# A decoder layer on one core: norm_mix as one row, spread over the partitions by two matmuls, and a written order for pre-norm and first projection

## Chip, cores and metric

One core of a Trainium2 chip runs the whole program. The metric is device time in microseconds (us) of one execution, as the median of several runs. TensorE is PE in the rows, VectorE DVE, ScalarE ACT, GpSimd POOL, SyncE SP.

## What is computed

A decoder layer on 512 tokens of width 1024, all in fp32. The part that matters here is its first line and the projection of it:

```python
def rms_norm(x, g):
    y = xf * lax.rsqrt(jnp.mean(xf * xf, axis=-1, keepdims=True) + NORM_EPS)
    return (y * g.astype(jnp.float32)).astype(x.dtype)
...
    xn = rms_norm(h, norm_mix[l])
    proj = xn @ w_in[l]                      # 1024 x 3128
    y_r = rwkv7_group(proj[..., :R_COLS], ...)
    y_n = nsa_group(proj[..., R_COLS:], positions, ...)
    h = h + jnp.concatenate([y_r, y_n], axis=-1) @ w_out[l]
    xn = rms_norm(h, norm_ffn[l])
    h = h + swiglu(xn, w_gate[l], w_up[l], w_down[l])
```

`rwkv7_group` is a linear recurrence over time in 8 heads; `nsa_group` is attention with compressed, selected and windowed keys, whose compression (`compress`) is a small MLP on blocks of 32 tokens: `silu(win @ w1 + b1) @ w2`. A final rms_norm ends the layer.

## The kernel before

Tokens lie in NT = 4 tiles of 128, the width in KB = 8 blocks of 128. Every fp32 operand of a product is split in a rounded high part (`split`: a copy on ACT to fp32r, L144) and the rest (a subtraction, on DVE at L146, or on POOL where asked), and `mm3` multiplies high by high, high by low and low by high (L163, L164, L165), so that a product of 128x512 is 3 matmuls for each block of the width.

The start: SP loads the first token tile in two halves, norm_mix, the first half of the weights `raw0`, tile 1, the second half, tiles 2 and 3, and `raw1`. TensorE runs 10 matmuls on the identity (WARM, L250) that nobody reads. For each token tile, `norm_transposed` sums the squares (ACT L173, L176), takes the root (L177), the reciprocal (DVE L178), multiplies the tile by it and by `gain` (norm_mix on all 128 partitions; one scalar_tensor_tensor, here STT, at L190; two of 512 columns for tile 0), transposes it block by block into two PSUM banks of tag "s" (PE L194), and splits each bank into `xh` (ACT) and `xl` (DVE). `proj_tok` then multiplies the tile by the 256 columns of w0, 24 matmuls of 256 columns. In this text T0 to T3 are the transposes of the four tiles, P0 to P3 these products, xh(1) the high parts of tile 1. After them the products of the remaining columns of w_in (128x512) follow, with the jobs that use them; among these are the sigmoids of `lora` products (L400 and L401 multiply, ACT L402 applies the sigmoid, DVE L405 scans), the sine and cosine of the rotary angles (ACT L360, L361), and `job_cmp1`, the first layer of the compression (DVE L660, ACT L661, DVE L662 make its operand `win`, PE L666 multiplies). The FFN combines blocks of w_gate and w_up by sums before it multiplies (`block4`, L1141 to L1145, with loads that add on arrival, issued by POOL).

A scheduler decides the order of the instructions on each engine at build time, from the order of the code, from its own estimates and from `tc.high_priority()`; on the chip each engine runs its list in order. A block `tc.manual_schedule(engines=...)` keeps the order of the code for the engines named. So an edit at the start changes the scheduler's lists also where the code is the same.

Of the kernel before, what the change touches and what calls it, by code (L numbers as in the profile page):

```python
# [17 lines left out]
S, D = 512, 1024  # L18
# [28 lines left out]
def hybrid_layer(ctx: ExitStack, tc: tile.TileContext, x, positions, norm_mix, w_in, mu_shift, w0, w2, a0, a2,  # L47
# [15 lines left out]
    def st(shape, tag, bufs=1, dtype=F32):  # L63
        return sb.tile(list(shape), dtype, name=tag, tag=tag, bufs=SB_BUFS.get(tag, bufs))
# [25 lines left out]
    gain = st([128, D], "t4")  # L90
# [4 lines left out]
    nc.sync.dma_start(gain, bcast_row(norm_mix))  # L95
# [85 lines left out]
    def norm_transposed(src, gain, hT, lT, halves=False):  # L181

        xn2 = st([128, 2, D], "b8")
        for t in range(NT):
            s = src(t)
            cut = (slice(0, 512), slice(512, D)) if halves and t == 0 else (slice(0, D),)
            r = rstd_of(s, cut)
            xn = xn2[:, t % 2]
            for c in cut:
                DVE.scalar_tensor_tensor(xn[:, c], s[:, c], r, gain[:, c], op0=OP.mult, op1=OP.mult)  # L190
            for k0 in range(0, KB, 4):
                p = ps("s")
                for k in range(4):
                    PE.transpose(p[:, k * 128:(k + 1) * 128], xn[:, (k0 + k) * 128:(k0 + k + 1) * 128], ident)  # L194
                pv = p.rearrange("p (k n) -> p k n", n=128)
                sl = slice(t * 128, (t + 1) * 128)
                split(pv, hT[:, k0:k0 + 4, sl], lT[:, k0:k0 + 4, sl])
            yield

# [49 lines left out]
    for _ in range(WARM):  # L249
        PE.matmul(idle[:, 0:128], ident, ident, start=True, stop=True)  # L250
    ident2 = st([128, 64], "ident2")
# [43 lines left out]
    norm = norm_transposed(lambda t: xt[:, t], gain, xh, xl, True)  # L295
    ctok = st([128, NT, 4, 64], "t4")
    for t in range(NT):
        next(norm)
        if t == 0:
            w0p = parts(raw0)  # L300
        ACT.activation(ctok[:, t].rearrange("p h d -> p (h d)"), proj_tok(w0p, t), AF.Copy)
    w1p = parts(raw1, lo_pool=True)
# [953 lines left out]
    for n, (a, b) in enumerate(GROUPS):  # L1256
        one, two = halves[n]
        a11, a21, a12, a22 = (h[:, :, x] for h in (one, two) for x in (left, right))
        first, last = n == 0, n == 1
        t1, t2 = block4(a, 0, "wraw"), block4(b, 1, ("gin", "kB")[n])  # L1260
        t3 = st([128, 4, 512], "wraw") if first else None
        t3 = [t3[:, 2 * i:2 * i + 2] if first else st([128, 2, 512], "t4") for i in range(2)]
# [4 lines left out]
        multiply(m1, a_side(a11), b_side(t1), first, last)  # L1267
# [7 lines left out]
        multiply(m5, a_side(a21), b_side(t1), first, last)  # L1275
# [84 lines left out]
```

## Time and profile before

| | |
|---|---|
| median of 3 runs | 760.38 us (759.34 to 761.85) |
| the profiled execution, its own time | 762.32 us |
| its span in the trace | 760.6 us |
| mean granted clock of TensorE | 0.981 of full |
| TensorE busy | 726.2 us, 95% |
| DVE, ACT, POOL busy | 593.1, 399.1, 164.6 us |

The span is what the trace shows of the profiled execution; the timed runs are other executions. Busy shares are of the span.

### The profile page before, as it was taken

The numbers are of one execution on the slowest core, as the hardware profiler recorded it, in microseconds if no ns is written. First come the engines' busy times: TensorE is split into PE (matmuls) and PEld (weight loads), VectorE is DVE, ScalarE is ACT, GpSimd is POOL, SyncE is SP. The second block draws the span as 40 slices with busy tenths as digits, with TensorE's granted clock in tenths as the row PEclk, the third lists the DMA queues.
The fourth block names the chain that finished last, engine by engine and source line by source line (L and its number), as shares of the span: only waits on it lengthen the run. The fifth ranks groups of instructions, "written<-read, shape, count | busy, mean of one in ns | idle before, by whom it ended". The sixth has DMA issues, their size and how long they took to land.

```text
span 760.6 us, 14951 instructions
## 1 busy us (share of the span) xinstructions
PE 726.2 (95%) x6045; PEld 636.6 (84%) x6045; DVE 593.1 (78%) x1089; ACT 399.1 (52%) x666; POOL 164.6 (22%) x262
## 2 busy tenths in 40 slices
PE   6999999998879999999998699999999999999996
PEld 6967878898867888767787699999999999877885
DVE  5488688879868888786459496969688789999835
ACT  6398735324366866756437534535344454465424
POOL 3210053048435542454001101111102001010000
PEclk7999999999999999999998999999999999999999
DMA  7723533100061000230415747695967629443302
GB/s 249 198 85 110 166 111 110 57 2 2 3 222 30 2 2 2 58 112 1 139 56 139 165 130 177 155 229 145 225 161 194 143 81 272 172 110 111 139 0 110
DMA packets 73467, 87.02 MB, mean 114 GB/s; under 512 B 4996, under 2 KB 62934, under 8 KB 73398
## 3 DMA queue, kind: packets, MB, share of 16 engines
q1 hardware_dynamic: 60694, 72.43, 29.2%
q0 software_dynamic: 12704, 13.63, 11.6%
q8 instruction: 47, 0.77, 0.4%
q14 instruction: 22, 0.18, 0.1%
HBM read 83.96 MB, written 2.10 MB: 113 GB/s over the span
## 4 chain that ended last, share of the span: by engine, by line
PE 67%; DVE 22%; DMA 4%; issue 3%; ACT 3%; POOL 0%; SPq 0%; DVEq 0%; ACTq 0%
PE ps_ra L164 6%; PE ps_ra L165 6%; PE ps_ra L163 6%; PE ps_pj L165 6%; PE ps_pj L163 6%; PE ps_pj L164 6%; PE ps_o L1001 3%; PE ps_s L165 3%; PE ps_s L163 3%; PE ps_s L164 3%; DVE wlo L146 3%; DVE L L146 3%; PE ps_pj L993 3%; DMA L<-in_w_up_dram 2%; DVE whi L146 2%
## 5 line engine op out<-in xcount | busy, mean ns | idle before, releaser
L144 ACT ACTIVATE whi<-wraw 128x1024 fp32r<-128x1024 f32 (+1 forms) x63 | 62.5, 1030 | 36.0 <-issue 9.1
L146 DVE TENSOR_TENSOR wlo<-wraw,whi 128x1024 fp32r<-128x1024 f32 (+1 forms) x46 | 58.9, 1306 | 16.3 <-ACT whi L144 12.8
L165 PE MATMUL ps_ra<-L,wlo 128*128 128x512 f32 (+2 forms) x144 | 50.9, 355 | 0.0
L990 POOL TENSOR_SCALAR whi<-whi,m,gates 128x128 f32<-128x128 f32 (+3 forms) x64 | 42.5, 680 | 37.1 <-DVE m L988 28.8
L164 PE MATMUL ps_ra<-L,whi 128*128 128x512 f32 (+2 forms) x136 | 47.4, 348 | 1.1 <-DVE L L146 1.1
L163 PE MATMUL ps_ra<-L,whi 128*128 128x512 f32 (+2 forms) x136 | 47.0, 346 | 1.2 <-ACT L L144 1.2
L164 PE MATMUL ps_pj<-L,whi 128*128 128x512 f32 (+1 forms) x128 | 45.7, 357 | 0.0
L163 PE MATMUL ps_pj<-L,whi 128*128 128x512 f32 (+1 forms) x128 | 45.1, 357 | 0.0
L165 PE MATMUL ps_pj<-L,wlo 128*128 128x512 f32 (+1 forms) x120 | 41.2, 343 | 0.0
L987 ACT ACTIVATE whi<-whi,m 128x128 f32<-128x128 f32 (+3 forms) x64 | 35.4, 554 | 9.5 <-DVE m L986 8.3
L163 PE MATMUL ps_ra<-whi,L 128*128 128x256 f32 (+1 forms) x108 | 35.7, 332 | 0.2 <-ACT L L144 0.2
L164 PE MATMUL ps_ra<-wlo,L 128*128 128x256 f32 (+1 forms) x108 | 35.7, 330 | 0.2 <-DVE wlo L146 0.2
L165 PE MATMUL ps_ra<-whi,L 128*128 128x256 f32 (+1 forms) x108 | 35.1, 327 | 0.0
L986 DVE CUSTOM_DVE_ANT_0 whi<-ps_s,negb 128x128 f32<-128x128 f32 (+3 forms) x64 | 29.3, 484 | 5.9 <-PE ps_pj L993 2.5
L165 PE MATMUL ps_pj<-whi,L 128*128 128x256 f32 (+1 forms) x108 | 33.9, 315 | 0.0
L164 PE MATMUL ps_pj<-wlo,L 128*128 128x256 f32 (+1 forms) x108 | 33.8, 313 | 0.0
L163 PE MATMUL ps_pj<-whi,L 128*128 128x256 f32 (+1 forms) x108 | 33.6, 315 | 0.0
L1141 POOL DMA_DIRECT2D t<-in_w_up_dram x6 | 7.9, 1323 | 114.0 <-DVE whi L146 50.2
L165 PEld LDWEIGHTS ps_ra<-L,wlo 128*128 128x128 f32 (+1 forms) x144 | 27.2, 189 | 4.2 <-issue 0.5
L164 PEld LDWEIGHTS ps_ra<-L,whi 128*128 128x128 f32 (+1 forms) x136 | 25.6, 188 | 4.8 <-DVE L L146 1.3
L163 PEld LDWEIGHTS ps_ra<-L,whi 128*128 128x128 f32 (+1 forms) x136 | 25.7, 189 | 4.7 <-ACT L L144 1.4
L164 PEld LDWEIGHTS ps_pj<-L,whi 128*128 128x128 f32 x128 | 24.9, 195 | 3.4 <-DVE L L146 0.4
(685 smaller groups left out, 2561.2 us busy)
## 6 DMA issues: line engine op xcount, KB each, us to landing
wraw<-in_w_gate_dram SPq DMA_DIRECT2D x22, 512.0 KB
wraw<-in_w_in_dram SPq DMA_DIRECT2D x9, 1024.0 KB
wraw<-in_w_down_dram SPq DMA_DIRECT2D x9, 1024.0 KB
t<-in_w_up_dram POOLq DMA_DIRECT2D x12, 512.0 KB, 7.4
wraw<-in_w_up_dram SPq DMA_DIRECT2D x11, 512.0 KB
L<-in_w_up_dram POOLq DMA_DIRECT2D x10, 512.0 KB, 8.2
wraw<-in_w_out_dram SPq DMA_DIRECT2D x4, 1024.0 KB
wraw<-in_w_in_dram SPq DMA_DIRECT2D x6, 512.0 KB
```

The source lines that it names most:

```text
L144: ACT.activation(hi, src, AF.Copy)
L146: (POOL if pool else DVE).tensor_sub(lo, src, hi.bitcast(F32))
L163: PE.matmul(o, lh, rh, start=start, stop=False)
L164: PE.matmul(o, lh, rl, start=False, stop=False)
L165: PE.matmul(o, ll, rh, start=False, stop=stop)
L986: DVE.tensor_tensor_reduce(pr[:, i], pS[:, i], negb[:, S - n:S], scale=-1.0, scalar=3e38, op0=OP.add, op1=OP.min, accum_out=m[:, i, 0:1])
L987: ACT.activation(pr[:, i], pr[:, i], AF.Exp, scale=-1.0, bias=m[:, i, 0:1], accum_out=m[:, i, 1:2])
L990: POOL.tensor_scalar(pr[:, i], pr[:, i], m[:, i, 2:3], gv[:, 1 + b0 + i, h:h + 1], op0=OP.mult, op1=OP.mult)
L993: PE.transpose(pT[:, j], prr[:, x, j * 128:j * 128 + 128], ident)
L1001: PE.matmul(po[q, 2 * g:2 * g + 2], vtok[:, j % (t + 1), b0 + j // (t + 1), g], pTs[:, par, j], start=False, stop=g == 1 and bs[-1] == 1 a ...
L1141: POOL.dma_start(t1, quarter(w_up, 0), accum_op=OP.add)
```

## The change

`gain` is no longer loaded to all partitions (128 times 4 KB): one row of 4 KB is loaded, and two fp32 matmuls behind WARM multiply it by a row of 128 ones, which leaves norm_mix on all partitions in two PSUM banks, of tags "rb" and "o". The STT reads its second operand from there, and is cut in two halves of 512 columns for all tiles. The loop over `norm_transposed` becomes a block with a written order for ACT and DVE. The low parts of w1 (two of 1024 columns) are made by DVE and no longer by POOL. Two variables of the FFN get other names.

```diff
-    gain = st([128, D], "t4")
+    gain_row = st([128, D], "t4")[0:1]
+    one = st([128, 256], "rp")[0:1, 0:128]
+    POOL.memset(one, 1.0)
...
-    nc.sync.dma_start(gain, bcast_row(norm_mix))
+    nc.sync.dma_start(gain_row, bass.AP(tensor=norm_mix.tensor, offset=norm_mix.offset, ap=[[D, 1], [1, D]]))
...
     idle = ps("o")
     for _ in range(WARM):
         PE.matmul(idle[:, 0:128], ident, ident, start=True, stop=True)
+    gain = [ps(o) for o in ("rb", "o")]
+    for f in range(2):
+        PE.matmul(gain[f], one, gain_row[:, f * 512:f * 512 + 512], start=True, stop=True)
...
-    norm = norm_transposed(lambda t: xt[:, t], gain, xh, xl, True)
     ctok = st([128, NT, 4, 64], "t4")
-    for t in range(NT):
-        next(norm)
-        if t == 0:
-            w0p = parts(raw0)
-        ACT.activation(ctok[:, t].rearrange("p h d -> p (h d)"), proj_tok(w0p, t), AF.Copy)
-    w1p = parts(raw1, lo_pool=True)
+    def rstd(t):
+        r[t] = rstd_of(xt[:, t], (slice(0, 512), slice(512, D)) if t == 0 else ())
+
+    def normed(t):
+        xn = xn2[:, t % 2]
+        for f in range(2):
+            c = slice(f * 512, f * 512 + 512)
+            DVE.scalar_tensor_tensor(xn[:, c], xt[:, t, c], r[t], gain[f], op0=OP.mult, op1=OP.mult)
+            p = turned[t, f] = ps("s")
+            for k in range(4):
+                PE.transpose(p[:, k * 128:(k + 1) * 128], xn[:, (f * 4 + k) * 128:(f * 4 + k + 1) * 128], ident)
+
+    def parted(t):
+        for f in range(2):
+            ks, tl = slice(f * 4, f * 4 + 4), slice(t * 128, t * 128 + 128)
+            split(turned[t, f].rearrange("p (k n) -> p k n", n=128), xh[:, ks, tl], xl[:, ks, tl])
+
+    def weights0(f):
+        ks = slice(f * 4, f * 4 + 4)
+        split(raw0[:, ks], w0p[0][:, ks], w0p[1][:, ks])
+
+    with tc.manual_schedule(engines={mybir.EngineType.Activation, mybir.EngineType.DVE}):
+        rstd(0)
+        normed(0)
+        weights0(0)
+        parted(0)
+        rstd(1)
+        normed(1)
+        weights0(1)
+        rstd(2)
+        parted(1)
+        for t in range(NT):
+            p = proj_tok(w0p, t)
+            if t < 2:
+                normed(t + 2)
+                if t == 0:
+                    rstd(3)
+                parted(t + 2)
+                if t == 1:
+                    w1p = parts(raw1)
+            ACT.activation(ctok[:, t].rearrange("p h d -> p (h d)"), p, AF.Copy)
```

The change adds lines to the file, so lines of the new one are other numbers: L190 answers to L294 there, L194 to L297, L144/L146 to L146/L148, L163 to L165 become L165 to L167, and from L304 on the new number is 25 higher (L666 is L691, L1145 is L1170).

What the scheduler makes of it is shown at three places. First DVE's list from its fourth instruction on, at the start of the program; `cneg` is a mask that the attention uses much later, `cvalid` what POOL makes for it. Before:

```order
L178 RECIPROCAL ss<-ss 128x1
L190 SCALAR_TENSOR_TENSOR b_165<-L,ss,t_69 128x512 x2
L283 TENSOR_SCALAR cneg<-cvalid 128x128
L146 TENSOR_TENSOR wlo<-wraw,whi 128x1024
L146 TENSOR_TENSOR L<-ps_s,L 128x4x128 x2
L178 RECIPROCAL ss<-ss 128x1
L190 SCALAR_TENSOR_TENSOR b_165<-L,ss,t_69 128x1024
```

After:

```order
L180 RECIPROCAL ss<-ss 128x1
L269 TENSOR_SCALAR cneg<-cvalid 128x128
L294 SCALAR_TENSOR_TENSOR b_170<-L,ss,ps_rb 128x512
L294 SCALAR_TENSOR_TENSOR b_170<-L,ss,ps_o 128x512
L148 TENSOR_TENSOR wlo<-wraw,whi 128x1024
L148 TENSOR_TENSOR L<-ps_s,L 128x4x128 x2
L180 RECIPROCAL ss<-ss 128x1
L294 SCALAR_TENSOR_TENSOR b_170<-L,ss,ps_rb 128x512
L294 SCALAR_TENSOR_TENSOR b_170<-L,ss,ps_o 128x512
L148 TENSOR_TENSOR wlo<-wraw,whi 128x1024
```

`cneg` stands behind the first two STTs in the list before and ahead of them in the list of the change; the rest is the written order.

Second, PE's list around the second `lora` products (L400, L401 before; L425, L426 after; `t_517` and `t_529` are the same operand) and the first compress product (L666, L691, its operand `t_757`, `t_769`). Before, the four `lora` products and what follows:

```order
L400 MATMUL ps_s<-b_518,t_517 128x512
L401 MATMUL ps_s<-b_518,t_517 128x512
L400 MATMUL ps_s<-b_518,t_517 128x512
L401 MATMUL ps_s<-b_518,t_517 128x512
L163 MATMUL ps_pj<-L,whi 128x512
L164 MATMUL ps_pj<-L,whi 128x512
L163 MATMUL ps_ra<-L,whi 128x512
L164 MATMUL ps_ra<-L,whi 128x512
L165 MATMUL ps_pj<-L,wlo 128x512
```

and the first compress product, 45 rows further on:

```order
L165 MATMUL ps_ra<-L,wlo 128x512
L163 MATMUL ps_ra<-L,whi 128x512
L164 MATMUL ps_ra<-L,whi 128x512
L165 MATMUL ps_ra<-L,wlo 128x512
L666 MATMUL ps_o<-whi,t_757 128x256
L666 MATMUL ps_o<-wlo,t_757 128x256
```

After:

```order
L425 MATMUL ps_s<-b_530,t_529 128x512
L426 MATMUL ps_s<-b_530,t_529 128x512
L425 MATMUL ps_s<-b_530,t_529 128x512
L426 MATMUL ps_s<-b_530,t_529 128x512
L691 MATMUL ps_o<-whi,t_769 128x256
L691 MATMUL ps_o<-wlo,t_769 128x256
```

The first compress product stands directly behind the `lora` products in the change's list; before, 45 products of 128x512 stand between them.

Third, DVE's list in the FFN, at the products that run near 434 us. `whi<-t_4545,whi` and `whi<-t_4557,whi` are the low part of the same operand; L1145 (L1170) sums two blocks that a load brings. Before:

```order
L146 TENSOR_TENSOR b_4728<-L,b_4728 128x4x128
L1196 TENSOR_TENSOR t_4805<-ps_s,t_4805 128x512
L1145 TENSOR_TENSOR L<-L,wraw 128x1024
L146 TENSOR_TENSOR whi<-t_4545,whi 128x1024
L1199 TENSOR_TENSOR t_4807<-ps_pj,t_4805 128x512
L146 TENSOR_TENSOR wlo<-wraw,wlo 128x1024
```

After:

```order
L148 TENSOR_TENSOR b_4740<-L,b_4740 128x4x128
L1221 TENSOR_TENSOR t_4817<-ps_s,t_4817 128x512
L148 TENSOR_TENSOR whi<-t_4557,whi 128x1024
L1170 TENSOR_TENSOR L<-L,wraw 128x1024
L1224 TENSOR_TENSOR t_4819<-ps_pj,t_4817 128x512
L148 TENSOR_TENSOR wlo<-wraw,wlo 128x1024
L148 TENSOR_TENSOR whi<-wraw,whi 128x1024
```

The low part stands ahead of L1170 in the change's list, and behind L1145 before.

## Rows read from the trace of the kernel before

**Rows 1.** The page of the profile: the span; part 1, busy time of PE; part 2, granted clock of PE, in tenths, in 40 slices of 19 us; part 4, the chain that ended last, by engine.

```profile
span 760.6 us, 14951 instructions
...
PE 726.2 (95%) x6045; PEld 636.6 (84%) x6045; DVE 593.1 (78%) x1089; ACT 399.1 (52%) x666; POOL 164.6 (22%) x262
...
PEclk7999999999999999999998999999999999999999
...
PE 67%; DVE 22%; DMA 4%; issue 3%; ACT 3%; POOL 0%; SPq 0%; DVEq 0%; ACTq 0%
```

**Rows 2.** The view of waits for PE in the first 34 us: what was waited for; total us, times, longest.

```profile
PE ps_s L194 <- DVE b L190: 3.7, 1, 3.7
```

**Rows 3.** The view of windows, five stretches of the start: length, busy us (and instructions) of PE, PEld, DVE, ACT, POOL, then granted clock of PE (1.00 is 2.4 GHz, 0.50 is 1.2 GHz), share of the DMA engines, GB/s.

```profile
5.55:8.03 2.48, 0.00 (x0) 0.00 (x0) 0.00 (x0) 0.00 (x0) 1.78 (x10) 1.00 0.98 328
8.03:11.44 3.41, 1.99 (x9) 1.59 (x9) 2.04 (x4) 1.61 (x3) 0.00 (x0) 0.50 1.06 398
11.44:14.86 3.42, 3.21 (x11) 2.62 (x12) 3.20 (x5) 3.42 (x6) 0.00 (x0) 0.50 1.04 370
14.86:18.27 3.41, 3.41 (x18) 3.41 (x17) 3.41 (x8) 3.12 (x9) 0.34 (x8) 0.50 0.36 116
18.27:22.00 3.73, 3.73 (x34) 3.73 (x33) 2.00 (x4) 2.57 (x4) 0.71 (x3) 1.00 0.05 11
```

**Rows 4.** Timeline of DVE: start us, us, engine, line, operation, out<-in, and in brackets the idle time before and what ended it.

```profile
5.38 0.16 DVE L178 RECIPROCAL ss<-ss 128x1 f32<-128x1 f32 x1 [1.18 <-ACT ss L177]
8.44 1.41 DVE L190 SCALAR_TENSOR_TENSOR b<-L,ss,t 128x512 f32<-128x512 f32 x2 [2.90 <-DMA t<-in_norm_mix_dram]
9.77 0.18 DVE L283 TENSOR_SCALAR cneg<-cvalid 128x128 bf16<-128x128 bf16 x1
13.72 1.28 DVE L190 SCALAR_TENSOR_TENSOR b<-L,ss,t 128x1024 f32<-128x1024 f32 x1
```

**Rows 5.** Timeline of ACT and of POOL, first stretch.

```profile
4.30 0.63 ACT L176 ACTIVATE t<-L 128x512 bf16<-128x512 f32 x1 [0.29 <-DMA L<-in_x_dram]
9.82 1.06 ACT L144 ACTIVATE whi<-wraw 128x1024 fp32r<-128x1024 f32 x1 [4.48 <-DMA wraw<-in_w_in_dram]
10.79 0.58 ACT L144 ACTIVATE L<-ps_s 128x512 fp32r<-128x512 f32 x1
7.59 0.12 POOL L281 MEMSET cvalid<- 128x4 bf16 x1
```

**Rows 6.** Timeline of PE, first stretch.

```profile
1.65 3.90 PE L250 MATMUL ps_o<-ident 128*128 128x128 f32 x20 [1.65 <-POOL ident L84]
9.25 1.97 PE L194 MATMUL ps_s<-ident,b 128*128 128x128 f32 x8 [3.70 <-DVE b L190]
...
16.87 0.56 PE L164 MATMUL ps_ra<-wlo,L 128*128 128x256 f32 x1
...
20.56 0.60 PE L194 MATMUL ps_s<-ident,b 128*128 128x128 f32 x4
```

**Rows 7.** The view of one line: the only fp32 matmuls with 512 columns in the trace, those of L882 (count: shortest, median, longest ns; first and last start).

```profile
L882 PE MATMUL ps_rb<-L,ones x8: 591/592/697, 241.6 to 332.9; 128*128 128x512 f32 x8
```

**Rows 8.** Timeline of ACT, then DVE, then PE around the second sigmoid batch and the first compress product.

```profile
60.30 0.61 ACT L439 ACTIVATE L<-gin 96x512 fp32r<-96x512 f32 x1
60.94 0.69 ACT L228 ACTIVATE t<-ps_pj,cs 128x512 f32<-128x512 f32 x1
62.80 1.28 ACT L360 ACT_TABLE_LOAD   x1
65.65 0.24 ACT L360 ACTIVATE t<-t 128x40 f32<-128x40 f32 x1 [1.56 <-DVE t L345]
69.79 1.27 ACT L402 ACTIVATE b<-ps_s,cs 128x512 f32<-128x512 f32 x2
72.65 1.21 DVE L405 TENSOR_TENSOR_SCAN b<-smask,b 128x512 f32<-128x512 f32 x1
71.66 1.07 DVE L660 TENSOR_TENSOR t<-t,t 128x496 f32<-128x496 f32 x1
75.07 0.67 DVE L662 TENSOR_TENSOR t<-t,t 128x496 fp32r<-128x496 f32 x1
66.58 0.49 PE L401 MATMUL ps_s<-b,t 64*128 64x512 f32 x1
77.58 0.28 PE L666 MATMUL ps_o<-whi,t 128*128 128x256 f32 x1
```

**Rows 9.** The view of waits for PE from 425 to 446 us, then the timeline of DVE and of PE there.

```profile
PE ps_pj L165 <- DVE whi L146: 3.3, 1, 3.3
434.98 1.23 DVE L1145 TENSOR_TENSOR L<-L,wraw 128x1024 f32<-128x1024 f32 x1 [5.79 <-DMA L<-in_w_up_dram]
436.12 1.22 DVE L146 TENSOR_TENSOR whi<-t,whi 128x1024 fp32r<-128x1024 f32 x1
437.25 0.69 DVE L1199 TENSOR_TENSOR t<-ps_pj,t 128x512 f32<-128x512 f32 x1
437.39 0.39 PE L165 MATMUL ps_pj<-L,whi 128*128 128x256 f32 x1 [3.26 <-DVE whi L146]
...
441.63 0.28 PE L164 MATMUL ps_ra<-L,wlo 128*128 128x256 f32 x1
```

**Rows 10.** The view of windows behind that wait, columns as in rows 3.

```profile
438.10:441.50 3.40, 3.40 (x19) 3.40 (x18) 3.40 (x5) 0.00 (x0) 0.00 (x0) 0.50 0.02 5
```

More of the change, by code (lines that the diff above doesn't have):

```diff
@@ L179, in rstd_of @@
         return ss[:, 2:3]
-    def norm_transposed(src, gain, hT, lT, halves=False):
-        xn2 = st([128, 2, D], "b8")
-        for t in range(NT):
[L185 to L198, printed above, removed]
     turn = [0]
@@ L294, in hybrid_layer @@
     xl = st([128, KB, S], "L", dtype=F32R)
-    norm = norm_transposed(lambda t: xt[:, t], gain, xh, xl, True)
+    xn2 = st([128, 2, D], "b8")
+    w0p = [st([128, 2048], tag, 2, F32R).rearrange("p (k n) -> p k n", n=256) for tag in ("whi", "wlo")]
     ctok = st([128, NT, 4, 64], "t4")
-    for t in range(NT):
-        next(norm)
-        if t == 0:
-            w0p = parts(raw0)
-        ACT.activation(ctok[:, t].rearrange("p h d -> p (h d)"), proj_tok(w0p, t), AF.Copy)
-    w1p = parts(raw1, lo_pool=True)
+    r, turned = {}, {}
+    def rstd(t):
[35 more added lines that the diff above has]
+            ACT.activation(ctok[:, t].rearrange("p h d -> p (h d)"), p, AF.Copy)
     pt = ps("s")
@@ L1258, in hybrid_layer @@
         a11, a21, a12, a22 = (h[:, :, x] for h in (one, two) for x in (left, right))
-        first, last = n == 0, n == 1
+        lead, end = n == 0, n == 1
         t1, t2 = block4(a, 0, "wraw"), block4(b, 1, ("gin", "kB")[n])
-        t3 = st([128, 4, 512], "wraw") if first else None
-        t3 = [t3[:, 2 * i:2 * i + 2] if first else st([128, 2, 512], "t4") for i in range(2)]
+        t3 = st([128, 4, 512], "wraw") if lead else None
+        t3 = [t3[:, 2 * i:2 * i + 2] if lead else st([128, 2, 512], "t4") for i in range(2)]
         for i in range(2):
@@ L1266, in hybrid_layer @@
         DVE.tensor_sub(a21, a22, a21)
-        multiply(m1, a_side(a11), b_side(t1), first, last)
+        multiply(m1, a_side(a11), b_side(t1), lead, end)
         DVE.tensor_add(a11, a21, a11)
@@ L1274, in hybrid_layer @@
             DVE.tensor_add(t2, t2, t1)
-        multiply(m5, a_side(a21), b_side(t1), first, last)
-        multiply(m6, a_side(a11), b_side(t2), first, last)
+        multiply(m5, a_side(a21), b_side(t1), lead, end)
+        multiply(m6, a_side(a11), b_side(t2), lead, end)
         DVE.tensor_sub(a21, a11, a22)
-        multiply(m7, a_side(a21), b_side(t3), first, last)
+        multiply(m7, a_side(a21), b_side(t3), lead, end)
     u, w, v = (st([128, 2, 512], tag) for tag in ("t4", "t4", "t4"))
```

## Prediction

> **What bounds the kernel now.** I read the page first. TensorE is busy 95% of a 760.6 us span, the chain that ended last lies 67% on it and 22% on VectorE (DVE), and the granted clock is full but in the first slice and a few short dips [rows 1]. So the end moves by what happens to TensorE's own stream: idle time in it, or time at 1.2 GHz. The view of waits gives the largest idle of the start: 3.7 us in which the first transposes wait for the first normalized tile [rows 2]. The timeline of DVE shows why: 1/rms is done at 5.54 (5.38 + 0.16), but the multiplication (STT) of L190 starts at 8.44, released by the transfer of norm_mix [rows 4]. The windows show what follows: TensorE does nothing from 5.55 to 8.03, and from 8.03 to 18.27 the clock is 0.50; in the last part of that, 14.86 to 18.27, it is busy all the time and still at half rate [rows 3]. It runs without a gap from 16.87 on [rows 6]. Everything after that start is a stream of products, so I then looked for places far behind where the new order of instructions adds or removes a wait of TensorE, and found two: the first compress product (L666, L691 in the new file), which does not wait today [rows 8], and the longest wait of the FFN's start, 3.3 us, followed by 3.4 us at clock 0.50 [rows 9, 10].
>
> **Part 1, the row.** The 512 KB broadcast becomes 4 KB behind the two halves of the first token tile. The second half is there at 4.30 [rows 5], so the row should be there before WARM ends at 5.55 (1.65 + 3.90, [rows 6]). Two fp32 matmuls follow. Their nearest rows are 592 ns each at full clock [rows 7]; those eight records belong to four matmuls (each fp32 product leaves two), so two matmuls are four records, between 1.7 us (pipelined, as the 0.39 us 128x512 matmuls overlap) and 2.4 us (end to end): the row would stand in PSUM at 7.3 to 8.0. At half clock throughout it would be up to 4.8 us, 10.3.
>
> But DVE does not start when the row is there. In the new order `cneg<-cvalid` stands ahead of the first STT (before, behind both). It reads cvalid, whose last memset on GpSimd (POOL) starts at 7.59 and takes 0.12 [rows 5]; one more small memset (`one`) is ahead of it on a busy POOL. So the first STT starts near 7.9, and the gain is 8.44 − 7.9 = 0.5 us, not 2.9. Upper bound of the gain, if POOL were early: 2.9 less the 1.7 of the matmuls, 1.2. Lower bound, at half clock: a loss of 1 us on the second half.
>
> **Part 2, the set order of the front.** From 7.9: two STTs until 9.3, transposes, xh on ACT 9.4 to 10.6, then the square of tile 1 ahead of nothing else, its reciprocal near 12.3, and the second tile's first STT at 12.4 instead of 13.72 [rows 4]. The first products of tile 1 (P1) now stand ahead of what remains of tile 0's 24 (P0), and need tile 1's xh, which ACT gives near 15.2. TensorE then runs without a gap from about 15.25 instead of 16.87: 1.6 us earlier. At 1.2 GHz until 18.27 those 1.6 us hold only half the work, worth 0.8; if the clock is already full, P0 and P1 are done 2.3 earlier (1.6 and the 1.4 us between 16.87 and 18.27 at half rate, halved).
>
> Against it: the transposes of tiles 2 and 3 came in fours among matmuls of other tiles (20.56, [rows 6]), so that ACT's and DVE's copies were hidden. Now eight transposes stand between P1 and P2 (and between P2 and P3) with nothing behind them but the product that reads them. TensorE waits for xh (0.58 copy, as at 10.79 [rows 5], with two hand-overs, less 0.4 of the second four transposes: about 0.45) and again for xl (0.69 on DVE less two short matmuls: about 0.5). Twice 0.95 is 1.9 us lost. The low parts of w1 moved from POOL to DVE cost nothing, since TensorE has P3 in front of them.
>
> Front in all: −2.3 + 1.9 = −0.4 if the clock is full early; −0.8 + 1.9 = about +1.2 at half rate until 18.27; and if it rises only one such stretch later, another 3.4 us at half rate [rows 3], worth 1.7: +2.9. I take +0.8, nearest the row that shows half rate while TensorE is busy.
>
> **The clock, weighed.** Rows 3 show it fall after 2.48 us of complete idleness and stay at 0.50 through 11.44 to 14.86 with TensorE 94% busy (3.21 of 3.42). "TensorE: Matmul & The Clock Gate" of the Trainium skill, Part 1, says that the throttled state is the default and that activity releases it. By that rule the two row matmuls, which fill the idle stretch, keep the rate up, and the front would be the −0.4 above; by the rows alone it is +1.2.
>
> **Part 3, the scheduler's other moves.** (a) In the new order the first compress product stands right behind the last L401 product, 45 products of 128x512 earlier. TensorE gets there at 67.0 (66.58 and 0.42), where it was 77.58 before [rows 8]. Its operand is made by DVE at the end of a chain: ACT L439 ends 60.91; a table load 1.28 and a sine 0.24 (now ahead of the sigmoids, behind them before); a copy 0.69; the other sine 0.24; a table load 1.28; the first of two sigmoids 0.64: 65.3. Then on DVE a scan 1.21, the sum L660 1.07, a short copy, a scan 1.21, the difference L662 0.67: 69.6, or 69.0 with the overlaps of 0.1 that consecutive starts show. Wait: 1.9 us (69.0 − 67.0). Lower bound 0, if the slack of later waits of TensorE takes it up; upper 1.9 + 1.7 with a clock drop like that in rows 10.
>
> (b) At the FFN's start DVE has L1145 at 434.98, released by a transfer, and behind it the low part `whi<-t` that TensorE wants; TensorE resumes at 437.39 [rows 9]. Now that low part stands ahead of L1145, and its inputs are there long before: the product runs at once, 22 matmuls at 0.12, from 434.0 to 436.6. The next operand, `wlo`'s low part, stands behind L1145 (to 436.12), L1199 (0.6) and its own 1.22: 437.9, a new wait of 1.3. The next product so starts at 437.9; at full rate before it would have been 437.39 + 2.64 = 440.0, so −2.1. It was in fact 441.63 [rows 9], the rest being 3.4 us at 0.50 [rows 10]: if the shorter wait no longer drops the clock, 1.7 more. I take half, −0.85. Bounds: 0 (the transfers bind later) and −3.8.
>
> (c) Elsewhere rows only change places by a few instructions; I allow +0.45 (0 to +0.9, the size of the single waits it could add in the attention part, like the xh wait above).
>
> **Sum.** +0.8 + 1.9 − 2.1 − 0.85 + 0.45 = +0.2 us. The profiled execution took 762.32 against a median of 760.38 of the three timed runs; the sum is a difference within the profiled one and goes on the median: 760.6.
>
> **Rivals.**
> *The clock stays up (faster).* The row matmuls fill the idle stretch, the front is −0.4; the FFN's shorter wait does not drop the clock, −3.8; L691's wait is 1.9 and (c) 0. For it: rows 10 show a drop only behind a wait of 3.3. Against it: half rate at 94% busy in rows 3. −0.4 − 3.8 + 1.9 = −2.3: 758.1; with L691's wait taken up later, 756.2.
> *The clock stays down (slower).* TensorE's holes behind the transposes of tiles 2 and 3, each 0.95, lie where it was gapless, and half rate lasts one stretch longer. Front +2.9 instead of +0.8: 762.7, and each further us at half rate adds 0.5. It decides from a rise at 21.7 on. For it: rows 3's stretch from 11.44 with short holes did not raise the clock; against it: TensorE is gapless from 15.25 until after P1.
> *The row doesn't do what it says.* `cneg`, or half-rate row matmuls, hold the first STT at 8.4 or later, so that the 512 KB saved are worth nothing: front +1.7 (1.2 + 0.5), 761.5: still no difference.
>
> **Numbers.** Chances: the forecast 0.36; the clock up 0.30; the clock down, or L691's wait with a clock drop (762.3 and more), 0.24; the row without effect 0.10. About ±2.3 us (0.3%) is what a measurement of this kernel can tell from no change. Faster 0.30, same 0.46, slower 0.24. The likeliest alone: 758.8 to 762.4. The range with both signs: 756.6 to 763.6, where the terms stand near their bounds on one side.
>
> **What would show it.** First STT near 7.9 behind `cneg`; TensorE gapless from 15.25; two waits of about 0.5 each behind the transposes of tiles 2 and 3; a wait of 1.9 at L691; at the FFN's start a wait of 1.3 in place of 3.3, and clock 1.00 or 0.50 behind it. I am wrong in the mechanism if the first STT starts before 7, if L691 does not wait, or if a clock dip somewhere between comes or goes: each is worth 1.7 us and I can't place them.

## The result and the profile after

The change made the kernel slower: 767.09 us (median of 6 runs, 763.55 to 769.20) against 759.75 us of the kernel before in the same session (6 runs, 757.51 to 761.85), a ratio of 1.0097 [1.0081, 1.0114], where 760.6 and a range up to 763.6 had been forecast. The profiled execution took 767.79 us against the 762.32 of before, 5.5 us more; its span is 766.1 us at a mean granted clock of 0.973 (0.981 before).

The page of the profile after, answering to [rows 1]: span, busy time, granted clock in 40 slices, the chain that ended last.

```profile
span 766.1 us, 14953 instructions
...
PE 737.0 (96%) x6049; PEld 641.0 (84%) x6049; DVE 600.4 (78%) x1094; ACT 400.1 (52%) x666; POOL 159.0 (21%) x261
...
PEclk8998999999999999999999899999999999999999
...
PE 70%; DVE 19%; ACT 4%; DMA 4%; issue 2%; POOL 1%; DVEq 0%; ACTq 0%; POOLq 0%; SPq 0%
```

TensorE is busy 10.8 us more for four more records, those of the row: it does the rest of its work more slowly. The clock's first slice is better than before, the lower one in the fourth slice (57 to 76 us) is new.

**The front** answers to [rows 2 to 6]. From the view of waits for PE in the first 34 us, the wait of the first transposes:

```profile
PE ps_s L297 <- DVE b L294: 1.1, 1, 1.1
```

Four windows of the start, the cuts after the first where the clock changes:

```profile
5.55:8.03 2.48, 2.11 (x6) 0.67 (x5) 0.27 (x3) 1.06 (x1) 1.87 (x11) 1.00 1.00 328
8.33:11.75 3.42, 2.94 (x12) 2.48 (x13) 3.21 (x5) 1.54 (x3) 0.00 (x0) 0.50 1.03 402
11.75:15.17 3.42, 3.42 (x16) 3.19 (x16) 2.71 (x5) 3.27 (x7) 0.00 (x0) 0.50 0.68 220
15.17:22.00 6.83, 6.32 (x50) 5.64 (x48) 3.76 (x10) 3.62 (x8) 0.74 (x10) 1.00 0.26 80
```

The timeline of DVE, first `cneg`, then the first STT of tile 0 and of tile 1:

```profile
7.88 0.20 DVE L269 TENSOR_SCALAR cneg<-cvalid 128x128 bf16<-128x128 bf16 x1 [2.21 <-POOL cvalid L267]
8.00 0.75 DVE L294 SCALAR_TENSOR_TENSOR b<-L,ss,ps_rb 128x512 f32<-128x512 f32 x1
...
13.00 0.75 DVE L294 SCALAR_TENSOR_TENSOR b<-L,ss,ps_rb 128x512 f32<-128x512 f32 x1
```

The timeline of PE: the row matmuls, the product from which it runs on, and the two waits behind the transposes of tile 2:

```profile
5.68 1.12 PE L236 MATMUL ps_rb<-t,rp 1*128 1x512 f32 x2
6.64 1.02 PE L236 MATMUL ps_o<-t,rp 1*128 1x512 f32 x2
...
15.89 0.39 PE L165 MATMUL ps_pj<-whi,L 128*128 128x256 f32 x1 [0.20 <-ACT L L146]
...
21.44 0.39 PE L165 MATMUL ps_ra<-whi,L 128*128 128x256 f32 x1 [0.25 <-ACT L L146]
22.17 0.39 PE L167 MATMUL ps_ra<-whi,L 128*128 128x256 f32 x1 [0.22 <-DVE L L148]
```

The row is in PSUM at 7.66, `cneg` holds DVE until 8.00, and the first STT comes 0.44 us earlier than before. The two waits behind the eight transposes of tile 2 add up to 0.47 us, and the clock is full from 15.17 instead of 18.27.

**The place at 68 us** answers to [rows 8]. The view of waits for PE from 60 to 90 us, where the kernel before has none:

```profile
PE ps_o L691 <- DVE t L210: 2.4, 1, 2.4
```

The windows behind that wait:

```profile
69.78:73.20 3.42, 2.28 (x11) 2.31 (x12) 3.34 (x6) 3.40 (x5) 0.00 (x0) 0.50 0.00 0
73.20:76.61 3.41, 3.41 (x13) 2.93 (x13) 3.36 (x4) 2.10 (x3) 0.16 (x1) 0.50 0.58 186
76.61:80.00 3.39, 3.39 (x16) 2.77 (x15) 3.39 (x6) 3.38 (x3) 0.00 (x0) 1.00 0.35 122
```

The timeline of ACT there:

```profile
64.73 1.28 ACT L427 ACT_TABLE_LOAD   x1
66.02 1.26 ACT L427 ACTIVATE b<-ps_s,cs 128x512 f32<-128x512 f32 x2
68.95 0.62 ACT L686 ACTIVATE t<-t 128x496 fp32r<-128x496 f32 x1 [1.66 <-DVE t L685]
69.47 1.99 ACT L146 ACTIVATE whi<-wraw 128x1024 fp32r<-128x1024 f32 x2
```

The timeline of DVE:

```profile
66.74 1.22 DVE L430 TENSOR_TENSOR_SCAN b<-smask,b 128x512 f32<-128x512 f32 x1 [3.44 <-ACT b L427]
67.89 1.03 DVE L685 TENSOR_TENSOR t<-t,t 128x496 f32<-128x496 f32 x1
69.00 1.20 DVE L430 TENSOR_TENSOR_SCAN b<-smask,b 128x512 f32<-128x512 f32 x1
70.14 0.64 DVE L687 TENSOR_TENSOR t<-t,t 128x496 fp32r<-128x496 f32 x1
70.92 2.36 DVE L148 TENSOR_TENSOR wlo<-wraw,whi 128x1024 fp32r<-128x1024 f32 x2
```

The timeline of PE, the last `lora` product and the first compress product:

```profile
68.04 0.49 PE L426 MATMUL ps_s<-b,t 64*128 64x512 f32 x1
70.92 0.55 PE L691 MATMUL ps_o<-whi,t 128*128 128x256 f32 x1 [2.39 <-DVE t L210]
```

The chain is the forecast one: table load, sigmoid, scan, sum, scan, difference. TensorE stands 2.4 us, from 68.53 to 70.92; the clock falls to 0.50 at 69.78, within this wait, and stays there for 6.83 us. The high parts of the next weights (`whi`), which the products after it need, come behind L686 in ACT's list.

**The FFN** answers to [rows 9, 10]. From the view of waits for PE from 420 to 446 us:

```profile
PE ps_ra L166 <- DVE L L148: 1.0, 1, 1.0
PE ps_ra L165 <- ACT L L146: 0.9, 1, 0.9
```

The window of the clock's dip there:

```profile
431.59:435.01 3.42, 3.42 (x18) 3.42 (x18) 2.16 (x4) 1.36 (x3) 0.00 (x0) 0.50 0.01 1
```

The timeline of DVE, the low part and the sum L1170:

```profile
440.06 1.23 DVE L148 TENSOR_TENSOR whi<-t,whi 128x1024 fp32r<-128x1024 f32 x1 [0.40 <-ACT whi L146]
444.16 1.23 DVE L1170 TENSOR_TENSOR L<-L,wraw 128x1024 f32<-128x1024 f32 x1 [2.87 <-DMA L<-in_w_up_dram]
```

The low part now stands ahead of the sum that waits for a transfer, and the wait of 3.3 us is gone. A dip of the clock, 3.4 us long, lies ahead of this place, at 431.59, instead of behind it. The two waits of 0.9 and 1.0 us just ahead of this dip do not explain it by themselves: at the same two products the kernel before waits a little longer (they end at 420.36 and 422.38) and stays at 1.00. Its view of waits for PE from 400 to 446 us:

```profile
PE ps_ra L163 <- ACT L L144: 1.2, 1, 1.2
PE ps_ra L164 <- DVE L L146: 1.1, 1, 1.1
```

**Where the 5.5 us lie.** To compare the two traces at equal work, I look for points at which TensorE has started the same number of records of each shape in both, the four records of the row left out, and read how much later the next record starts in the change:

| point | before, us | after, us | later by |
|---|---|---|---|
| behind the front | 55.35 | 56.33 | 0.98 |
| at the last `lora` products | 66.15 | 67.61 | 1.46 |
| behind the first compress product | 79.49 | 85.92 | 6.43 |
| behind the attention | 367.89 | 375.63 | 7.74 |
| ahead of the wait of rows 9 | 433.73 | 444.24 | 10.51 |
| behind its dip | 444.03 | 449.56 | 5.53 |
| in the FFN | 467.68 | 473.12 | 5.44 |
| end of the span | 760.62 | 766.09 | 5.47 |

So the change is 1.0 us later behind the front; it loses 5.4 around the compress product and 1.3 from there to 368 us, gains 2.3 from 368 to 468 us, and is as late at the end as it is there. A single trace fixes the first of these terms badly: six other kernels below have the same front, and at the point of 55 us they are between 0.2 us earlier and 2.2 us later than the kernel before.

**A second difference is everywhere.** In the FFN's last part, where no wait and no dip lies in either trace, TensorE gets through fewer products in equal time. The view of windows, 700 to 750 us, of the kernel before (PE's busy time and instructions come first):

```profile
700.00:750.00 50.00, 50.00 (x222) 41.44 (x221) 31.57 (x35) 21.25 (x28) 0.00 (x0) 1.00 0.19 70
```

The same window of the change:

```profile
700.00:750.00 50.00, 50.00 (x216) 40.42 (x215) 31.14 (x32) 19.26 (x23) 0.00 (x0) 1.00 0.21 74
```

The mean distance from one 128x512 product to the next is there 226.7 ns before and 232.8 ns after, at the same full clock; that of the 128x256 products, over the whole trace, is 119.2 and 118.8 ns. The prediction has no word of it.

### The profile page after: what moved, and what is told of

Its sections match the earlier page's. It is cut to its first block, busy times and chain, and to the rows that moved or that the text cites. A ratio compares the mean times of both kernels' runs of the same rounds, so it can differ in the third digit from the quotient of the medians.

```text
span 766.1 us, 14953 instructions
## 1 busy us (share of the span) xinstructions
PE 737.0 (96%) x6049; PEld 641.0 (84%) x6049; DVE 600.4 (78%) x1094; ACT 400.1 (52%) x666; POOL 159.0 (21%) x261
## 4 chain that ended last, share of the span: by engine, by line
PE 70%; DVE 19%; ACT 4%; DMA 4%; issue 2%; POOL 1%; DVEq 0%; ACTq 0%; POOLq 0%; SPq 0%
PE ps_ra L165 6%; PE ps_ra L167 6%; PE ps_pj L167 6%; PE ps_ra L166 6%; PE ps_pj L166 6%; PE ps_pj L165 6%; PE ps_s L165 4%; PE ps_s L167 4%; PE ps_s L166 4%; DVE wlo L148 3%; PE ps_o L1026 2%; DMA L<-in_w_up_dram 2%; PE ps_pj L1018 2%; DMA L<-in_w_gate_dram 1%; DVE t L582 1%
## 5 line engine op out<-in xcount | busy, mean ns | idle before, releaser
L146 ACT ACTIVATE whi<-wraw 128x1024 fp32r<-128x1024 f32 (+1 forms) x63 | 62.7, 1031 | 38.3 <-issue 11.4
L148 DVE TENSOR_TENSOR wlo<-wraw,whi 128x1024 fp32r<-128x1024 f32 (+1 forms) x48 | 61.8, 1312 | 18.5 <-ACT whi L146 17.2
L167 PE MATMUL ps_ra<-L,wlo 128*128 128x512 f32 (+2 forms) x144 | 50.9, 354 | 0.0
L165 PE MATMUL ps_ra<-L,whi 128*128 128x512 f32 (+2 forms) x136 | 48.1, 355 | 0.9 <-ACT L L146 0.9
L165 PE MATMUL ps_pj<-L,whi 128*128 128x512 f32 (+1 forms) x128 | 45.3, 359 | 0.1
L167 PE MATMUL ps_pj<-L,wlo 128*128 128x512 f32 (+1 forms) x120 | 42.2, 351 | 0.1
L165 PE MATMUL ps_ra<-whi,L 128*128 128x256 f32 (+1 forms) x108 | 35.2, 326 | 0.2 <-ACT L L146 0.2
L167 PE MATMUL ps_ra<-whi,L 128*128 128x256 f32 (+1 forms) x108 | 35.0, 324 | 0.2 <-DVE L L148 0.2
L165 PE MATMUL ps_pj<-whi,L 128*128 128x256 f32 (+1 forms) x108 | 34.3, 319 | 0.5 <-ACT L L146 0.5
L167 PE MATMUL ps_pj<-whi,L 128*128 128x256 f32 (+1 forms) x108 | 33.9, 316 | 0.2 <-DVE L L148 0.2
L167 PEld LDWEIGHTS ps_ra<-L,wlo 128*128 128x128 f32 (+1 forms) x144 | 26.7, 186 | 4.7 <-issue 0.5
L165 PEld LDWEIGHTS ps_ra<-L,whi 128*128 128x128 f32 (+1 forms) x136 | 26.2, 193 | 4.6 <-ACT L L146 1.2
L165 PEld LDWEIGHTS ps_pj<-L,whi 128*128 128x128 f32 x128 | 24.6, 192 | 4.0 <-ACT whi L146 0.4
```

The source lines that it names most:

```text
L146: ACT.activation(hi, src, AF.Copy)
L148: (POOL if pool else DVE).tensor_sub(lo, src, hi.bitcast(F32))
L165: PE.matmul(o, lh, rh, start=start, stop=False)
L167: PE.matmul(o, ll, rh, start=False, stop=stop)
```

## The experiments

Ratios go against the kernel before, run beside each kernel on the same chip.

| kernel | us | ratio |
|---|---|---|
| after, compress product late | 769.82 | 1.0136 [1.0114, 1.0159] |
| before, compress product early | 771.31 | 1.0147 [1.0122, 1.0172] |
| row alone (old loop) | 757.47 | 0.9958 [0.9940, 0.9977] |
| order alone (broadcast kept) | 770.53 | 1.0136 [1.0102, 1.0171] |
| new front, lists of before behind it | 764.51 | 1.0055 [1.0028, 1.0083] |
| new front, lists of the row alone | 763.91 | 1.0046 [1.0021, 1.0071] |
| old front, lists of after behind it | 766.81 | 1.0082 [1.0048, 1.0116] |
| after, weights' parts first | 772.58 | 1.0155 [1.0131, 1.0179] |
| before, weight tiles 128 bytes lower | 763.56 | 1.0021 [1.0000, 1.0042] |
| after, weight tiles where before has them | 765.44 | 1.0052 [1.0028, 1.0076] |
| new front, lists of the row alone, tiles as before | 758.70 | 0.9972 [0.9945, 1.0000] |
| row alone, weight tiles +128 bytes | 763.85 | 1.0031 [1.0013, 1.0048] |
| row alone, weight tiles +256 bytes | 758.83 | 0.9977 [0.9955, 1.0000] |
| row alone, all tiles +96 bytes | 758.44 | 0.9981 [0.9961, 1.0002] |
| row alone, all tiles +224 bytes | 760.80 | 1.0001 [0.9978, 1.0023] |
| row alone, all tiles +128 bytes | 759.57 | 0.9980 [0.9957, 1.0002] |

**1. Is it the place of the first compress product?** My first theory. In the change it is held behind the last product of the next projection; in the kernel before it is put ahead of that projection.

```diff
+                if half == 1:   # after: order edge, no semaphore
+                    tc.add_manual_dep(T["cmp"], T["pe"].ins.name, DependencyInfo(NoSync, DATA), reason="order")
```

```diff
+                with tc.issue_after(T["cmp"].ins) if half else nullcontext():   # before
+                    p = proj_tile(w, j * 128)
```

> The changed kernel, with one edge of order added: the first compress product (L691 there) is issued behind the second v product, as in the kernel before. Theory A (the early compress product is the loss: 2.4 us of wait and half rate from 69.8 to 76.6 in the changed kernel's trace, about 5.2 us together): 761.9, within 0.4% of before, no wait of TensorE at the compress product. Theory B (the front itself, row and written order, is the loss): it stays at 766 to 767. Theory C (the rest of the reshuffled lists is the loss, spread over the attention part): somewhere at 764 to 767, and its clock dips elsewhere.

> The kernel before, with one edge of order added: the second v product is issued behind the first compress product, so that this one stands right behind the lora products as in the changed kernel. Front untouched. Theory A: slower than before by about 5 us, 765, with a wait of TensorE of 2 us or more at the compress product and a clock of 0.50 near 70 us. Theory B: no difference, 760. Theory C: in between, without a wait there.

The early product alone costs the kernel before 11 us; its wait is longer than that of the change. The view of waits for PE from 60 to 95 us in this kernel:

```profile
PE ps_o L668 <- DVE t L227: 8.8, 1, 8.8
```

The window of the dip, which begins within that wait (66.45 to 75.25) and outlasts it:

```profile
67.97:78.21 10.24, 2.96 (x14) 2.99 (x15) 7.05 (x11) 8.56 (x8) 0.91 (x2) 0.50 0.34 102
```

But the late product gives the change nothing back. From the view of waits for PE, 60 to 95 us, in the change with the late product:

```profile
PE ps_pj L165 <- ACT whi L146: 2.0, 1, 2.0
```

TensorE now stands for the weights of the next projection, which ACT still makes behind L686, and the clock is 0.50 from 72.57 to 75.98. At equal work this kernel loses 4.4 us between 55 and 79 us, where the change loses 5.4. The place of this product is sufficient for a loss, but in the change it is not the only thing that is late: the theory falls in this form.

**2. Each half alone.** The row with the old loop, and the written order with the broadcast load.

```diff
+    gain_row = st([128, D], "t4")[0:1]          # row alone; norm_transposed kept,
+            for f in range(2):                  # its STT in two halves from PSUM
```

```diff
-    gain = [ps(o) for o in ("rb", "o")]         # order alone
+    gain = [gain_all[:, 0:512], gain_all[:, 512:1024]]
```

> The kernel before with the row and the two fp32 matmuls alone: the old loop of the pre-norm, its order left to the scheduler, the multiplication reads PSUM in two halves. Here the compress product stands late, as in the kernel before. Theory A: 759 to 761, as before. Theory B with the row as its cause: 766 to 767; with the written order as its cause: 760. Theory C: its DVE list behind the front is close to that of the changed kernel (152 rows differ, against 434 from before), so 764 to 767.

> The changed kernel with the broadcast load of before: no row, no fp32 matmuls, the written order of pre-norm and first projection kept. Here the compress product stands early, as in the changed kernel. Theory A: 765 to 767, with the wait at the compress product. Theory B with the row as its cause: 760; with the written order as its cause: 766 to 767, lost before 45 us. Theory C: its lists behind the front are close to those of before, so 760 to 762.

The order carries the loss, with the same wait of 2.4 us at the compress product and the clock at 0.50 from 71.19 to 78.01. The row alone is the fastest kernel here, though its front is no faster (1.9 us later at equal work): like the kernel before it has no wait near 68 us, and it gains 3.2 us between 368 and 468 us and 2.5 behind that.

**3. The front or the lists behind it?** The order of the instructions behind the front is now taken from another build: each engine's instructions there are chained by order edges (without semaphores) in the sequence of the other.

```diff
+    mark = len(nc.cur_bb.bb.instructions)       # behind the front
...
+    pin(tc, nc, mark, TABLE)                    # TABLE: each engine's sequence in the other build
```

> The changed kernel's front (row, fp32 matmuls, written order) with everything behind the front pinned, on every engine, to the lists of the kernel before. Theory C (the loss is made by the reshuffled lists behind the front, whatever the front does): 759 to 761, within 0.3% of before, and nothing of the waits at 68 to 71 us. Theory B (the front itself loses): 765 to 767.

> The front of the kernel before (broadcast load, scheduler's order) with everything behind it pinned to the lists of the changed kernel. Theory C: 765 to 768, with TensorE's waits behind the second pair of lora products and the clock at 0.50 there. Theory B: 760.

> The changed kernel's front with the lists behind it pinned to those of the run with the row alone (which took 757.5). In the profiled executions that run's front stood 0.9 us behind the changed kernel's at 44 us, and its lists gained from there on. Theory C: 756 to 758, the fastest so far; theory B: above 760.

With the old front and the lists of after, the wait (`PE ps_o L690 <- DVE t L250`, 2.4 us), the dip (70.40 to 77.22) and a loss of 5.6 us between 55 and 79 us are all back: the loss at 68 us belongs to the lists. With the new front and either of the other lists no wait is left there, and behind the front they are 0.7 us later and 0.2 us earlier than the kernel before. Yet these two are still 0.5% slower than before, not equal as a loss from lists alone would have it. In both, the 128x512 products come every 232.4 to 232.9 ns; with the old front and the new lists, every 226.7.

**4. The weights' parts first.** In the lists of after, ACT's two `whi` parts go ahead of L686, DVE's `wlo` behind the first scan, and the compress product behind the projection.

> The changed kernel with its own lists pinned and three moves in them: on ScalarE the two high parts of the second v product's weights ahead of the copy L686 (one row up), on VectorE their two low parts behind the first scan of the second batch (five rows up), on TensorE the first compress product behind the second v product. Theory D (at 68 us both products that could run wait, one for the sigmoids and scans, the other for the weights' parts that stand behind them, so that moving the compress product alone gains nothing): the wait behind the lora products falls from 2.4 to under 0.5, the clock does not drop there, 761 to 762. If the time stays at 766 to 767, the place at 68 us is not what costs.

The wait at 68 us is gone (0.6 us lost between 55 and 77 us), and a new one stands 20 us later, in front of the second half of the compress product. From the view of waits for PE, 60 to 95 us:

```profile
PE ps_o L715 <- DVE t L233: 3.2, 1, 3.2
```

The timeline of ACT, two makings of `whi` and L710, the L686 of this file, for each half of the compress product:

```profile
68.27 2.00 ACT L169 ACTIVATE whi<-wraw 128x1024 fp32r<-128x1024 f32 x2
72.80 0.62 ACT L710 ACTIVATE t<-t 128x496 fp32r<-128x496 f32 x1 [2.53 <-DVE t L709]
...
80.98 2.01 ACT L169 ACTIVATE whi<-wraw 128x1024 fp32r<-128x1024 f32 x2 [5.83 <-issue]
...
87.94 0.60 ACT L710 ACTIVATE t<-t 128x496 fp32r<-128x496 f32 x1
```

`whi` has two buffers, and the compress product reads one of them. ACT stands 5.83 us before it makes the weights after next, and starts when the projection's last product runs (80.74); that fits the other buffer coming free, though the profile names no releaser. The operand of the second half (87.94) comes behind these weights in ACT's list. Three moves by hand do not mend lists of several hundred.

**5. What slows the 128x512 products?** In experiment 3, kernels with the same lists behind the front differ in pace. What differs in the built programs is where tiles lie: memory is allotted in the order in which tags first appear in the code, and the written order allots the weights' tiles (`w0p`, tags whi and wlo) before the first `rstd` allots the norm's small tile `ss`, 4 buffers of 32 bytes. So whi and wlo start at byte 183584 of a partition in the change and at 183712 in the row alone (182560 in the order alone and 182688 before, where the 1 KB of tag rp is not allotted this early).

```diff
+    w0t.extend(st([128, 2048], tag, 2, F32R) for tag in ("whi", "wlo"))   # before: ahead of ss
```

```diff
-    w0p = [st([128, 2048], tag, 2, F32R)... for tag in ("whi", "wlo")]    # after: moved
     rstd(0)
+    w0p = [st([128, 2048], tag, 2, F32R)... for tag in ("whi", "wlo")]    # behind ss
```

In these three kernels the lists are held as in experiment 3, so that only the addresses differ.

> The kernel before, every list unchanged, row for row; the only difference is where tiles lie in SBUF: the 128 bytes of the norm's small tile ss are allotted behind the weights' tiles whi and wlo instead of ahead of them, so that whi and wlo start 128 bytes lower, as in the changed kernel (where the written order allots the weights first). Theory E (the start addresses of whi and wlo set the pace of the products, seen as 232.7 ns for one 128x512 matmul against 226.7 in the traces): 128x512 at 232 to 233 ns, 128x256 at 118.7 instead of 119.7, about 2 us slower, 762 to 764. Otherwise (the pace belongs to the order): 226.7 ns and 760.5.

> The changed kernel, every list unchanged, row for row; the weights' tiles are allotted behind the first rstd(0), so that whi and wlo lie as many bytes above a multiple of 512 as in the kernel before. Theory E: 128x512 at 226 to 227 ns, 765 (2 us below the changed kernel's 767). Otherwise 232 ns and 767.

> The changed kernel's front, the lists of the row-alone run behind it, and the weights' tiles where the kernel before has them relative to 512 bytes. Theory E: it takes back 2 to 4 us of the 763.9 of the same lists with the tiles lower, and since its front stood about 2 us ahead of the row-alone run's in the traces, it may reach 756 to 760. If addresses do not matter, 764.

The pace follows the tiles each time: 233.3 ns with before's own lists and the tiles lower, 226.7 in the two with the tiles put back. The window 700 to 750 us of the kernel before with the tiles lower, answering to the 222 above:

```profile
700.00:750.00 50.00, 50.00 (x216) 40.19 (x216) 31.33 (x34) 19.91 (x27) 0.00 (x0) 1.00 0.18 64
```

**6. The place itself, or the distance?** The row alone with its lists unchanged row for row; only a small tile is wider. Widening `ss` moves whi and wlo and what is allotted behind them; widening `eps` moves all tiles behind it together, L (xh, xl) among them.

```diff
-        ss = st([128, 4], "ss", 4)
+        ss = st([128, 16], "ss", 4)             # +128; 24 for +256
```

```diff
-    eps_t = st([128, 3], "eps")
+    eps_t = st([128, 27], "eps")                # +96; 59 for +224, 35 for +128
```

> The kernel with the row alone, its lists of instructions unchanged row for row; the small tile of the norm is 48 bytes wider in each of its four buffers, so whi and wlo and what is allotted behind them start 128 bytes higher (whi at 183840, 32 above a multiple of 512), and the other operand's tiles (L) stay. Theory 1 (the pace of the 128x512 products hangs on the place of whi and wlo against the place of L, in steps of 256 bytes: 256 apart gave 226.7 ns, 128 apart 232.7): 128 apart again, so 232 to 233 ns and 760 to 762 us, against 757.47 for the row alone. Theory 2 (the place of whi and wlo by itself, 288 above a multiple of 512 being a bad one): a new place, 226.7 or anything else. Theory 3 (the pace went with something else than the addresses): 226.7 ns and 757.5.

> As the kernel with the tiles 128 bytes higher, but 256 bytes higher (whi at 183968, 160 above a multiple of 512). Theory 1: whi and L a whole multiple of 512 apart, which is 256 apart in steps of 256: 226.7 ns and 757.5 us. Theory 2: open, another value than for plus 128. If the pace falls from step to step with no period, both are wrong.

> The row alone, lists unchanged, the small tile eps 96 bytes wider, so that all tiles behind it start 96 bytes higher: L at 4864, whi at 183808, a whole multiple of 512; the distance of the two is as in the row alone. Theory 1: 226.7 ns and 757.5 us. Theory 2 (own place): another pace; if a start on a whole multiple is what helps, towards 213 ns (512 columns at 2.4 GHz), which over some 1,100 such matmuls would be 15 us less, 743.

> The row alone, lists unchanged, all tiles behind eps 224 bytes higher: L at 4992, whi at 183936, 128 above a multiple of 512; their distance as in the row alone. Theory 1: 226.7 ns and 757.5 us, the same as plus 96. Theory 2: a pace of its own, and a different one from plus 96.

> The row alone, lists unchanged, eps 128 bytes wider, so that all tiles behind it start 128 bytes higher: whi at 183840, the very place that gave 233 ns when whi and wlo moved alone, and L at 4896, their distance as in the row alone. Theory 1 (the distance of the two operands): 226.7 ns, 222 or 223 PE instructions in 700 to 750 us, and a time like the three other kernels of that pace, 757.5 to 760.8 us. Theory 2 (the place itself, 32 above a multiple of 256): 233 ns, 216 instructions, 762 to 764 us.

The window of 700 to 750 us in the row alone:

```profile
700.00:750.00 50.00, 49.64 (x220) 40.76 (x218) 30.86 (x37) 18.51 (x28) 0.00 (x0) 1.00 0.22 83
```

With the weight tiles 128 bytes higher:

```profile
700.00:750.00 50.00, 50.00 (x216) 40.40 (x215) 30.80 (x34) 20.97 (x27) 0.00 (x0) 1.00 0.18 65
```

With the weight tiles 256 bytes higher:

```profile
700.00:750.00 50.00, 50.00 (x223) 41.40 (x222) 31.01 (x36) 20.93 (x29) 0.00 (x0) 1.00 0.20 74
```

With all tiles 128 bytes higher:

```profile
700.00:750.00 50.00, 50.00 (x222) 41.42 (x221) 31.01 (x35) 19.91 (x28) 0.00 (x0) 1.00 0.20 74
```

The row alone had 220 with 0.36 us of TensorE idle. The last kernel has whi at the very address of the second (183840) and the pace of the first: 226.7 ns against 233.0. All tiles +96 and +224 gave 226.7 too. So for the steps tried here the place itself does not count; the distance between whi and wlo and the tiles allotted ahead of them does: in all eighteen kernels, before and after among them, a whole multiple of 256 bytes between whi and L gave 226.7 ns, and 128 bytes more 232.4 to 233.3. In the traces of before and after it is the products of an L tile with a whi or wlo tile, some 1,000 in each, whose median distance goes from 227 to 232 ns. That the reads of these two tiles are the ones that meet is not shown, since the L tiles moved with all the others.

## Why the prediction was wrong

**The clock, weighed, and Part 1 and 2 (front, +0.8): near.** `cneg` held the first STT as said (8.00 for 7.9), the row matmuls took 1.98 us (1.7 to 2.4), and TensorE runs on from 15.89 (15.25). At tile 2's transposes the change is 1.6 us ahead at equal work (20.92 against 22.52), four records later 0.6 (22.39 against 22.99): this pair of waits, 0.47 us of idle time, costs 1.0 where 0.95 was said. The term came out as +1.0. With the spread of the same front in the other traces, −0.2 to +2.2, that it is so near is partly luck. "TensorE: Matmul & The Clock Gate" of the Trainium skill, Part 1, has activity release the throttle: the trace agrees in half. During the row matmuls (2.11 us busy of 2.48) the clock was 1.00, and yet it fell at 8.33 and stayed at 0.50 through 3.42 us in which TensorE was never idle. It rose 3.1 us earlier than before. The rival "clock stays down" did not happen.

**Part 3(a), L691's wait (+1.9, at most 3.6): this step failed, by size.** Place, chain and releaser were right; the wait was 2.4. The term was 5.4 (5.0 from the last `lora` products on), because the clock drop, which I kept for the upper bound and priced at 1.7 after [rows 10], came, and lasted 6.83 us: TensorE was busy 2.28 + 3.41 = 5.69 us of it, half of which is lost, 2.85. 2.4 + 2.85 = 5.25. And the slack of later waits took nothing up: the change is still 6.7 later at 110 us. The rows at hand said 3.3 us of wait and a drop [rows 9, 10], and 3.7 us of wait and a drop [rows 2, 3]. The trace of the kernel before had two more that the prediction did not use, waits near 2 us; the view of waits for PE over the whole span, and the window behind the first of them, which ends at 407.37:

```profile
PE ps_s L1086 <- ACT L L1088: 2.0, 1, 2.0
PE ps_s L630 <- ACT b L623: 2.3, 2, 1.7
...
407.40:414.20 6.80, 5.44 (x24) 5.14 (x25) 6.80 (x10) 5.52 (x11) 1.32 (x1) 0.50 0.75 209
```

Behind the wait of 1.7 us the clock is 0.50 too, from 185.52 to 188.93. So all four waits over 1.5 us in that trace, the program's first wait at 0 to 1.65 apart, go with a drop, and so does one of 1.0 (it ends at 109.32, the clock is 0.50 from 110.43); a wait of 1.9 without one was not what these rows made likely. Nor did I see that the weights behind the product were late by as much, so that the product's place was not the whole of it (experiments 1 and 4).

**Part 3(b), the FFN (−2.1, and −0.85 for the clock): right at the place, not around it.** At the place itself the change gains 5.0: the wait went entirely, 3.4, without the new 1.3, since all is later by then and the transfers were in, and the dip behind it went too, 1.6. But from 368 to 434 us it loses 2.8, of which 1.5 in the new dip at 431.59. The net is −2.3. Why that dip came, at waits no longer than those of the kernel before, stays open.

**Part 3(c), elsewhere (+0.45, at most 0.9).** +1.3 in the trace, up to 368 us, and nothing behind 468. The sign of being wrong that I could not place, a dip that comes or goes, did occur: the change is at 0.50 from 226.8 to 233.6, where the kernel before is not. It cost only 0.4, since TensorE waits there in both traces. Spread over all terms is what the prediction lacks altogether: **the slower 128x512 products**. A trace has some 1,000 of them and 2,400 of 256 columns, so 1,000 x 6.1 ns − 2,400 x 0.5 ns = 4.9 us, an estimate from the paces above and an upper one, since waits of TensorE take part of it up. Measured in pairs with equal lists: 0.0021, 0.0045, 0.0074 of the time (experiment 5: before, after, the row's lists), 1.6 to 5.6 us, the first of them hardly clear of nothing; and 1.0031 against 0.9958 to 1.0001 in experiment 6. The single traced executions of the three pairs differ by 0.8, 1.0 and 2.2 us. Nothing in the profile of before could have shown this, but the two built programs did: the addresses were there to be compared.

**The sum.** In the forecast's terms the trace has +1.0 for the front, +5.4 for L691's wait, −2.3 for the FFN and +1.3 elsewhere, where +0.8, +1.9, −2.95 and +0.45 were said: L691's wait is more than half of the error of 5.3. (The sum for half rate, −0.8 + 1.9, is +1.1 and not +1.2, which changes nothing.) The runs divide the loss another way. The change with its tiles put back stays at 1.0052, so that of its 1.0% some 0.45% goes with the place of the tiles and some 0.5% with lists and front. The old front with the new lists costs 0.8%, which agrees within the intervals. The new front against another one, with equal lists and tiles, shows no effect of one sign: 1.0052 against 1.0082, 0.9972 against 0.9958, 1.0055 against 1.0021. What the place at 68 us is worth by itself is read from traces, in four kernels that have it; no kernel here mends it alone. Open also is why the change makes up some 3 us in the middle of the attention and loses them again by 368 us.

**The best version.** The row alone at 757.47 us, and the new front with the row's lists and the tiles at the old distance at 758.70, beat both kernels in the median. But four kernels with the row's lists and its pace, at other addresses, gave 758.44 to 760.80: most of the five ratios lie near 0.998, so that the gain is rather 1.5 us than 3.

## What to carry to other kernels

An edit at the start of a scheduled program is an edit of all its lists: compare them for the places where a product now comes ahead of the work that makes its operand, and price each new wait together with the clock drop that goes with it, and do not leave the drop to the upper bound. Compare the addresses of the two builds as well as their lists. And when two kernels differ by 1%, count products in an equal stretch without waits first: 222 against 216 says at once that it is not only a matter of waiting.

## What the runs showed of the hardware

A 128x512 fp32r product came every 226.7 ns, or every 232.4 to 233.3, by nothing but 128 bytes between tiles; one of 256 columns went the other way, 119.2 and 118.8. "SBUF — State Buffer" of the Trainium skill, in "A bandwidth-pool intuition that's wrong (but worth ruling out)", gives TensorE a second independent read port for loading its stationary operand, the one that stays in the array. I would have concluded from it that the distance of the two operands does not matter; no run here shows which reads meet, but the measured pace does depend on where the tiles lie.

A wait of 2.4 us brought 6.83 us at half rate in four kernels (the change, the same with its tiles put back, the order alone, the old front with the new lists), and one of 8.8 us 10.24; one of 3.2 us (experiment 4) brought 3.41, at 89.54. In the kernel before, 2.0 us brought 6.8 and 1.7 us 3.4; a wait of 1.73 us that ends at 194.36 in the kernel with the early product brought none. So the price behind a wait is not read from its length alone.

Two fp32 matmuls of one row by 512 columns took 1.12 and 1.02 us at full clock, near the 2 x 0.59 of [rows 7] with all 128 rows: a row is not cheaper for having only one partition.
